# An output projection in column groups: low parts of the weights, residual loads, PSUM banks and gating in another order

## The chip, the core and the metric

The kernel runs on one core of a Trainium2 chip. The metric is the device time of one execution in microseconds (us). PE is the engine of the matmuls, DVE VectorE, ACT ScalarE, POOL GpSimd and SP SyncE; each works through its own instructions in order, and the DMAs that it issues stand in that order too. PSUM is the memory that PE writes to; the kernel uses it as eight banks of 128 partitions by 512 float32.

## What is computed

Two layers are applied to 640 tokens (128 context tokens and 512 latent ones), each 2048 wide. Per layer, with `h` the modulated input:

```python
shift, scale, gate = jnp.split(silu(cond) @ ada_w_l + ada_b_l, 3)
h = x * (1 + scale) + shift
z = h @ w_in_l
mix = concat([att * silu(ag), hg_out * silu(hgate), cv_out * silu(cgate)])
out = mix @ w_out_l                                  # (640, 2048) @ (2048, 2048)
x_new = layer_norm(ALPHA * x + gate * out, ln_w_l, ln_b_l)
```

This document is about the last two lines. `gate` and ALPHA scale the product and the residual `x`; the normalised result is the next layer's `x`, or the output.

## The kernel before, in words

Every large product is made with float32 accuracy from a high and a low part of each operand: `hi` is the operand rounded to float32r, `lo` is the operand minus `hi`, and three matmuls (HH by hi, HH by lo, HL by hi) are summed in PSUM. HH and HL hold the high and low parts of the activations for 5 token tiles (TT) and 16 steps of the contraction (KT). The layers follow each other: an input projection of 52 column tiles with the mixers' work beside it, then the output projection.

The **output projection** (lines 1411 to 1485) goes through 2048 output columns in five column groups, `GROUPS` (line 62): three of 512 columns (groups 0, 1, 2) and two of 256 (groups 3, 4). In groups 0 to 3 the loop of line 1417 takes the contraction step k outermost and the five token tiles inside, three matmuls each (line 1424), so five PSUM banks are open at once. Group 4 (lines 1460 to 1484) takes the token tiles outermost (line 1466), so that each tile can go on into the layer norm as soon as its 16 steps are done. A step k makes 15 matmuls.

**Weights.** `w_out` comes as 64 tiles of 128 x 512 a layer: 16 for each 512-wide group (a tile is a step k) and 8 for each 256-wide one (a tile is two steps). `o_load` (1143) loads a tile into one of the 8 RAW buffers on the SP queue. `o_split` (1149) makes hi and lo in two of the 16 WH buffers by `split_add` (288): ACT casts hi from RAW, ACT writes minus hi into lo, and POOL issues a DMA that adds the tile to lo once more from HBM. `feed` (1271) is called when a step has given its WH buffers back: it splits as many tiles as there are free pairs (so eight tiles are in flight) and loads until five are ahead of the split. RAW comes back after the cast.

**Work beside it in layer 0.** `ada_dve` (336) computes the next layer's modulation on DVE from 256 KB tiles (adawD) loaded on SP into the same RAW buffers. `pump(1, RWO)` after each step k (line 1430) lets it do RWO steps, and a step is two multiply-and-sum instructions of line 361 with their accumulator reads. With RWO = 1 that is 16 steps in each group. While five weight tiles are held, the three RAW buffers left let one ada tile be in flight at a time (line 343). In layer 1 there is no such work left.

**The residual.** `load_y` (1299) loads 128 tokens of `x` over all 2048 columns, 1 MB, on the POOL queue; the five of a layer are issued in group 0 after the steps 3, 5, 7, 9 and 11 (line 1431). In layer 1 `x` is the normalised value without weight and bias, and `affine` (1316) multiplies and adds them on DVE, from rows that `rows` (1306) loads on SP together with the gates. Those of group 0 are loaded at its start, those of each next group after step 9 of the group before; after step 13 of group 0 `affine` does groups 0 and 1, and after step 13 of the groups 1 to 3 the group that follows.

**Gating.** After step 15, `y_gate` (1326) multiplies each bank by the gate into a buffer, which is what gives the bank back; `y_add` (1332) then adds ALPHA times the residual and takes statistics (`bn_stats`). Both are on DVE, behind all that DVE was given in the group.

**PSUM banks** are taken from a queue (lines 1304, 1415, 1442): the four tiles m0 to m3 of one bank, then the two halves of each of the two-bank tiles z0 and z1, `free` being the halves of the one that the last input tile did not use. Five are taken per group and put back at its end, so a group begins with the three that its predecessor left, and the first pass over steps 0 and 1 does three token tiles before the other two (line 1418). In groups 1 and 3 the first bank so taken is the other half of a z tile whose first half the group before used for its last token tile.

**The end.** In layer 0 the tiles of group 4 are normalised, transposed and split into HH and HL (`ln_norm`, `ln_next`). In layer 1 `ln_out` (1395) normalises and stores the output.

Of the kernel before, what the change touches and what calls it, by code (L numbers as in the profile page):

```python
# [17 lines left out]
P = 128  # L18
D = 2048
KT = 16  # L20
T = 640
TT = 5
# [22 lines left out]
W0 = 4  # L45
WN = (0, 3, 4)
CY = 5
RWO = 1.0
WKEEP = 3
FL = 3  # L50
HF = 3
# [73 lines left out]
def trunk(ctx: ExitStack, tc: tile.TileContext, A: dict):  # L125
# [162 lines left out]
    def split_add(hi, lo, r, w):  # L288
        act.copy(hi, r)  # L289
        act.activation(lo, hi.bitcast(F32), AF.Copy, scale=-1.0)  # L290
        pool.dma_start(out=lo, in_=w.bitcast(F32R), accum_op=ALU.add)  # L291
# [857 lines left out]
    def o_split(l, t):  # L1149
        pump_until(lambda: len(WH.f) >= 2)  # L1150
        hi, lo = WH.take(), WH.take()
        r = oraw.pop((l, t))
        split_add(hi, lo, r, A["wout"][l, t])
        osp[l, OT[t][0], OT[t][1]] = (hi, lo)
        RAW.put(r)

# [57 lines left out]
    for l in range(DEPTH):  # L1214
# [81 lines left out]
        Y = yt["y"].rearrange("p (t n) -> p t n", t=TT)  # L1296
        xsrc = A["xr"] if l == 0 else n0

        def load_y(tt):
            pool.dma_start(out=Y[:, tt, :], in_=xsrc[128 * tt:128 * tt + 128, :])  # L1300

        zh = [z[:, h:h + 512] for z in zt for h in (0, 512)]
        free = [t[:, h:h + 512] for t in zt if t.tensor.name != z.tensor.name for h in (0, 512)]
        banks = deque(mb + free + [z[:, h:h + 512] for h in (0, 512)])

        def rows(gi):
            n0c, w = GROUPS[gi]
            src = [gsc[l, c] for c in range(2)] + ([A["lnw_r"][l - 1], A["lnb_r"][l - 1]] if l else [])
            out = []
            for r in src:  # L1310
                s = S.take()
                sync.dma_start(out=s[:, 0:w], in_=r[n0c:n0c + w].partition_broadcast(P))
                out.append(s)
            return out

        def affine(gi, gb):
            n0c, w = GROUPS[gi]
            for t in range(TT) if gi == 0 else (slice(0, TT),):
                yv = Y[:, t, n0c:n0c + w]
                for s, op in zip(gb[2:], (ALU.mult, ALU.add)):  # L1320
                    r = s[:, 0:w]
                    dve.tensor_tensor(yv, yv, r if gi == 0 else r.unsqueeze(1).to_broadcast([P, TT, w]), op=op)
            S.put(*gb[2:])
            del gb[2:]

        def y_gate(gi, tt, b, gb):
            w = GROUPS[gi][1]
            t = S.take()
            dve.tensor_tensor(t[:, 0:w], b[:, 0:w], gb[0 if tt == 0 else 1][:, 0:w], op=ALU.mult)  # L1329
            return t  # L1330
# [81 lines left out]
        gnext = None  # L1412
        for gi, (n0c, w) in enumerate(GROUPS[:-1]):
            gb = gnext or rows(gi)
            bs = [banks.popleft() for _ in range(TT)]
            kper = 512 // w
            for k0 in range(0, KT, 2):
                for tts, k in [(p, k) for p in ((range(3), range(3, TT)) if k0 == 0 else (range(TT),))
                               for k in (k0, k0 + 1)]:
                    hi, lo = osp[l, gi, k // kper]  # L1420
                    o = w * (k % kper)
                    for tt in tts:
                        for n_, (h_, w_) in enumerate(((HH, hi), (HH, lo), (HL, hi))):
                            pe.matmul(bs[tt][:, 0:w], lhsT=h_[:, tt, k, :], rhs=w_[:, o:o + w],  # L1424
                                      start=(k == 0 and n_ == 0), stop=(k == KT - 1 and n_ == 2))
                    if TT - 1 in tts:
                        if k % kper == kper - 1:
                            WH.put(*osp.pop((l, gi, k // kper)))
                            feed()
                        pump(1, RWO)  # L1430
                if gi == 0 and k0 in (2, 4, 6, 8, 10):
                    load_y(k0 // 2 - 1)
                if k0 == 8 and last:
                    gnext = rows(gi + 1)
                if k0 == 12 and last:
                    if gi == 0:
                        affine(gi, gb)
                    affine(gi + 1, gnext)
            ts = [y_gate(gi, tt, bs[tt], gb) for tt in range(TT)]
            for tt in range(TT):  # L1440
                y_add(gi, tt, ts[tt])
            banks.extend(bs)
            S.put(*gb)
        gi = len(GROUPS) - 1
        w = GROUPS[gi][1]
        gb = gnext or rows(gi)
        if last:
            cells = [RAW.take() for _ in range(8)]
            fin = [cells[0:4], cells[4:8]]
            for f, nm in zip(fin, ("lnw_r", "lnb_r")):  # L1450
                for q in range(4):
                    sync.dma_start(out=f[q], in_=A[nm][l, 512 * q:512 * q + 512].partition_broadcast(P))
        else:
            pump_until(lambda: not adaq)
            affine_consts()
            w_load(l + 1, 0)
            w_load(l + 1, 1)
            obank = [mb[0], zh[1], zh[3], zh[1], zh[3]]
            banks = deque(mb[1:] + mb[:1])
        for tt in range(TT):  # L1460
            b = banks.popleft() if last else obank[tt]
            for k in range(KT):
# [138 lines left out]
```

## Time and profile before

| | us |
|---|---|
| median of 3 runs (2290.06 to 2292.2) | 2291.16 |
| the profiled execution, its own time | 2289.98 |
| its span | 2288.2 |
| PE busy in the span | 2185.4 (96%) |
| DVE / ACT / POOL busy | 1393.0 / 1216.5 / 700.6 |
| output projection, layer 0, about | 928 to 1150 |
| output projection, layer 1, about | 2027 to 2284 |

Times in the rows are us from the start of the span. "Idle before" is the time that an engine stood still before an instruction, with the instruction that ended it. A busy share says how much of the time an engine had something to do; what a change can win is read from the waits of the engine that sets the pace in that stretch, here PE, and at the very end DVE.

### The profile page before, as it was taken

The numbers are of one execution on the slowest core, as the hardware profiler recorded it, in microseconds if no ns is written. First come the engines' busy times: TensorE is split into PE (matmuls) and PEld (weight loads), VectorE is DVE, ScalarE is ACT, GpSimd is POOL, SyncE is SP. The second block draws the span as 40 slices with busy tenths as digits, with TensorE's granted clock in tenths as the row PEclk, the third lists the DMA queues.
The fourth block names the chain that finished last, engine by engine and source line by source line (L and its number), as shares of the span: only waits on it lengthen the run. The fifth ranks groups of instructions, "written<-read, shape, count | busy, mean of one in ns | idle before, by whom it ended". The sixth has DMA issues, their size and how long they took to land. (4 is left out here: it accounts for less than half of the span.)

```text
span 2288.2 us, 42327 instructions
## 1 busy us (share of the span) xinstructions
PE 2185.4 (96%) x15854; PEld 2080.8 (91%) x15854; DVE 1393.0 (61%) x3647; ACT 1216.5 (53%) x2163; POOL 700.6 (31%) x790
## 2 busy tenths in 40 slices
PE   5899999999999999979989999999999999997996
PEld 3699999999999999868879999999999999996886
DVE  3488889557679998544473666534655786123227
ACT  1177877546564335623355878754656533552332
POOL 0034335322212333312232334433222224332225
PEclk9999999999999999989999999999999999998998
DMA  9968878887768789989835777678776667687884
GB/s 370 396 185 199 196 191 200 209 206 174 180 144 193 189 182 258 278 222 209 190 130 134 159 170 169 155 184 195 156 153 125 131 152 171 150 213 206 174 165 121
DMA packets 225663, 434.04 MB, mean 190 GB/s; under 512 B 26192, under 2 KB 32048, under 8 KB 223536
## 3 DMA queue, kind: packets, MB, share of 16 engines
q0 software_dynamic: 76544, 147.38, 37.7%
q1 hardware_dynamic: 138992, 271.85, 37.5%
q10 hardware_dynamic: 9920, 12.10, 1.6%
q8 instruction: 124, 2.03, 0.4%
q14 instruction: 83, 0.68, 0.1%
HBM read 413.87 MB, written 12.11 MB: 186 GB/s over the span
## 5 line engine op out<-in xcount | busy, mean ns | idle before, releaser
L1171 PE MATMUL z<-HH,wh 128*128 128x384 f32 x3296 | 1046.7, 339 | 0.0
L1169 PE MATMUL z<-HH,wh 128*128 128x256 f32 x3296 | 926.0, 283 | 1.1 <-DVE wh L286 0.9
L291 POOL DMA_DIRECT2D wh<-win x388 | 344.7, 934 | 1098.5 <-ACT wh L290 1017.0
L1169 PEld LDWEIGHTS z<-HH,wh 128*128 128x128 f32 x3296 | 619.0, 188 | 5.0 <-DVE wh L286 1.6
L1171 PEld LDWEIGHTS z<-HH,wh 128*128 128x128 f32 x3296 | 620.5, 188 | 1.5
L361 DVE SCALAR_TENSOR_TENSOR junk<-raw,s 128x256 bf16<-128x256 f32 x1024 | 502.5, 491 | 140.1 <-DMA raw<-adawD 111.9
L1171 PE MATMUL z<-HL,wh 128*128 128x384 f32 x1648 | 557.9, 339 | 0.0
L289 ACT CAST wh<-raw 128x512 fp32r<-128x512 f32 x516 | 316.1, 613 | 326.7 <-PE m L1424 131.1
L1169 PE MATMUL z<-HL,wh 128*128 128x256 f32 x1648 | 461.2, 280 | 0.0
L290 ACT ACTIVATE wh<-wh 128x512 fp32r<-128x512 f32 x516 | 326.4, 632 | 84.2 <-PE z L1171 69.5
L1169 PEld LDWEIGHTS z<-HL,wh 128*128 128x128 f32 x1648 | 310.6, 188 | 0.0
L1171 PEld LDWEIGHTS z<-HL,wh 128*128 128x128 f32 x1648 | 310.2, 188 | 0.0
L1026 DVE SCALAR_TENSOR_TENSOR s<-s,sm,s 128x655 f32<-128x655 f32 x240 | 229.0, 954 | 6.3
L291 POOL DMA_DIRECT2D wh<-wout x128 | 110.3, 862 | 347.1 <-ACT wh L290 336.2
L1424 PE MATMUL m<-wh,HH 128*128 128x512 f32 (+1 forms) x768 | 205.0, 354 | 0.0
L1424 PE MATMUL z<-wh,HH 128*128 128x512 f32 (+1 forms) x512 | 154.5, 384 | 29.8 <-DVE s L1329 28.4
L1424 PEld LDWEIGHTS m<-wh,HH 128*128 128x128 f32 x768 | 136.0, 189 | 19.8
L1424 PEld LDWEIGHTS z<-wh,HH 128*128 128x128 f32 x512 | 96.1, 193 | 49.3 <-issue 27.5
L1424 PE MATMUL m<-wh,HL 128*128 128x512 f32 (+1 forms) x384 | 135.8, 354 | 0.0
L1095 ACT ACTIVATE s<-z 128x640 f32<-128x640 f32 x32 | 22.5, 704 | 150.4 <-PE z L1171 141.6
L1424 PE MATMUL z<-wh,HL 128*128 128x512 f32 (+1 forms) x256 | 97.7, 382 | 0.0
L361 DVE DVE_READ_ACCUMULATOR junk<-raw,s 128x1 f32 x1024 | 83.5, 82 | 0.0
(555 smaller groups left out, 2661.0 us busy)
## 6 DMA issues: line engine op xcount, KB each, us to landing
raw<-win SPq DMA_DIRECT2D x416, 256.0 KB, 4.3
wh<-win POOLq DMA_DIRECT2D x388, 256.0 KB, 5.5
raw<-adawD SPq DMA_DIRECT2D x256, 256.0 KB, 4.2
x<-adaw SPq DMA_DIRECT2D x64, 512.0 KB, 8.2
raw<-wout SPq DMA_DIRECT2D x128, 256.0 KB, 5.0
wh<-wout POOLq DMA_DIRECT2D x128, 256.0 KB, 5.7
s<-crow SPq DMA_DIRECT2D x32, 256.0 KB, 6.2
s<-xT ACTq DMA_DIRECT2D x16, 320.0 KB, 7.1
```

Of the source, the lines that this page charges most:

```text
L289: act.copy(hi, r)
L290: act.activation(lo, hi.bitcast(F32), AF.Copy, scale=-1.0)
L291: pool.dma_start(out=lo, in_=w.bitcast(F32R), accum_op=ALU.add)
L361: dve.scalar_tensor_tensor(junk, r[:, 256 * n:256 * n + 256], 1.0, rows[0][:, 256 * c:256 * c + 256], op0=ALU.mult, op1=ALU.mult, accum_ou ...
L1026: dve.scalar_tensor_tensor(acc, u[:, t:t + AW], sm[:, cw + t:cw + t + 1], acc, op0=ALU.mult, op1=ALU.add)
L1095: act.activation(s[:, 0:T], zsb(z), AF.Silu)
L1169: pe.matmul(za, lhsT=w_, rhs=h_[:, 0:2, k, :], start=st_, stop=sp_)
L1171: pe.matmul(zb, lhsT=w_, rhs=h_[:, 2:5, k, :], start=st_, stop=sp_)
L1424: pe.matmul(bs[tt][:, 0:w], lhsT=h_[:, tt, k, :], rhs=w_[:, o:o + w], start=(k == 0 and n_ == 0), stop=(k == KT - 1 and n_ == 2))
```

## The change

Six edits, all in the output projection.

- From the seventh weight tile on (ODMA = 6) `o_split` calls `split`: ACT casts hi, and DVE subtracts hi from the loaded tile. Minus hi on ACT and the adding DMA go. RAW then comes back after the subtraction.
- `load_y` loads one column group of 128 tokens (512 columns, 256 KB; for group 3 the 512 columns of groups 3 and 4) after the steps 1, 3, 5, 7 and 9 of groups 0 to 3.
- `affine` is done for each group at its own step 11, per token tile; the rows are loaded at the group's start, and those of group 4 are loaded and used at step 11 of group 3, behind group 3's own.
- The banks are queued as m0, m1, the two `free` halves, m2, the two other halves, m3, and the last group's banks are chosen to match.
- After the steps 14 and 15 `feed` is not called; it is called once behind the five `y_gate`, ahead of `y_add`.
- RWO = 4/3 in the steps 0 to 11 and 0 in the steps 12 to 15: still 16 steps a group.

```diff
@@ -45,7 +45,8 @@
 W0 = 4
 WN = (0, 3, 4)
 CY = 5
-RWO = 1.0
+RWO = 4 / 3
+ODMA = 6
 WKEEP = 3
 FL = 3
 HF = 3
@@ -1150,7 +1151,10 @@
         pump_until(lambda: len(WH.f) >= 2)
         hi, lo = WH.take(), WH.take()
         r = oraw.pop((l, t))
-        split_add(hi, lo, r, A["wout"][l, t])
+        if t < ODMA:
+            split_add(hi, lo, r, A["wout"][l, t])
+        else:
+            split(hi, lo, r)
         osp[l, OT[t][0], OT[t][1]] = (hi, lo)
         RAW.put(r)
 
@@ -1296,12 +1300,16 @@
         Y = yt["y"].rearrange("p (t n) -> p t n", t=TT)
         xsrc = A["xr"] if l == 0 else n0
 
-        def load_y(tt):
-            pool.dma_start(out=Y[:, tt, :], in_=xsrc[128 * tt:128 * tt + 128, :])
+        def load_y(gi, tt):
+            n0c, w = GROUPS[gi]
+            w = w if gi + 2 < len(GROUPS) else 2 * w
+            if gi + 1 < len(GROUPS):
+                pool.dma_start(out=Y[:, tt, n0c:n0c + w], in_=xsrc[128 * tt:128 * tt + 128, n0c:n0c + w])
 
         zh = [z[:, h:h + 512] for z in zt for h in (0, 512)]
-        free = [t[:, h:h + 512] for t in zt if t.tensor.name != z.tensor.name for h in (0, 512)]
-        banks = deque(mb + free + [z[:, h:h + 512] for h in (0, 512)])
+        zf = [t[:, h:h + 512] for t in zt if t.tensor.name != z.tensor.name for h in (0, 512)]
+        zl = [z[:, h:h + 512] for h in (0, 512)]
+        banks = deque(mb[0:2] + zf + mb[2:3] + zl + mb[3:4])
 
         def rows(gi):
             n0c, w = GROUPS[gi]
@@ -1315,11 +1323,10 @@
 
         def affine(gi, gb):
             n0c, w = GROUPS[gi]
-            for t in range(TT) if gi == 0 else (slice(0, TT),):
+            for t in range(TT):
                 yv = Y[:, t, n0c:n0c + w]
                 for s, op in zip(gb[2:], (ALU.mult, ALU.add)):
-                    r = s[:, 0:w]
-                    dve.tensor_tensor(yv, yv, r if gi == 0 else r.unsqueeze(1).to_broadcast([P, TT, w]), op=op)
+                    dve.tensor_tensor(yv, yv, s[:, 0:w], op=op)
             S.put(*gb[2:])
             del gb[2:]
 
@@ -1412,6 +1419,7 @@
         gnext = None
         for gi, (n0c, w) in enumerate(GROUPS[:-1]):
             gb = gnext or rows(gi)
+            gnext = None
             bs = [banks.popleft() for _ in range(TT)]
             kper = 512 // w
             for k0 in range(0, KT, 2):
@@ -1426,25 +1434,29 @@
                     if TT - 1 in tts:
                         if k % kper == kper - 1:
                             WH.put(*osp.pop((l, gi, k // kper)))
-                            feed()
-                        pump(1, RWO)
-                if gi == 0 and k0 in (2, 4, 6, 8, 10):
-                    load_y(k0 // 2 - 1)
-                if k0 == 8 and last:
-                    gnext = rows(gi + 1)
-                if k0 == 12 and last:
-                    if gi == 0:
+                            if k0 < KT - 2:
+                                feed()
+                        pump(1, RWO if k0 < 12 else 0.0)
+                if k0 < 10:
+                    load_y(gi, k0 // 2)
+                if k0 == 10:
+                    if last:
                         affine(gi, gb)
-                    affine(gi + 1, gnext)
+                    if gi + 2 == len(GROUPS):
+                        gnext = rows(gi + 1)
+                        if last:
+                            affine(gi + 1, gnext)
             ts = [y_gate(gi, tt, bs[tt], gb) for tt in range(TT)]
+            feed()
             for tt in range(TT):
                 y_add(gi, tt, ts[tt])
             banks.extend(bs)
             S.put(*gb)
         gi = len(GROUPS) - 1
         w = GROUPS[gi][1]
-        gb = gnext or rows(gi)
+        gb = gnext
         if last:
+            banks = deque(mb[2:3] + zl[:1] + mb[3:4] + mb[0:2])
             cells = [RAW.take() for _ in range(8)]
             fin = [cells[0:4], cells[4:8]]
             for f, nm in zip(fin, ("lnw_r", "lnb_r")):
@@ -1455,8 +1467,8 @@
             affine_consts()
             w_load(l + 1, 0)
             w_load(l + 1, 1)
-            obank = [mb[0], zh[1], zh[3], zh[1], zh[3]]
-            banks = deque(mb[1:] + mb[:1])
+            obank = [mb[2], zh[1], zh[3], zh[1], zh[3]]
+            banks = deque(mb[3:] + mb[:3])
         for tt in range(TT):
             b = banks.popleft() if last else obank[tt]
             for k in range(KT):
```

## Rows read from the trace of the kernel before

**Rows 1.** Waits of PE, 920:1200 us (output projection, layer 0): total, times, longest.

```profile
PE z L1424 <- DVE s L1329: 15.0, 2, 13.3
...
PE m L1466 <- DMA wh<-wout: 1.8, 2, 1.2
```

**Rows 2.** Waits of PE, 2020:2289 us (output projection, layer 1).

```profile
PE z L1424 <- DVE s L1329: 13.4, 1, 13.4
...
PE z L1424 <- ACT wh L290: 1.4, 1, 1.4
```

**Rows 3.** Timeline of PE around the end of column group 0, layer 0 (start, duration).

```profile
982.47 0.39 PE L1424 MATMUL z<-wh,HL 128*128 128x512 f32 x1
996.16 1.19 PE L1424 MATMUL z<-wh,HH 128*128 128x512 f32 x2 [13.30 <-DVE s L1329]
...
1001.05 0.63 PE L1424 MATMUL z<-wh,HH 128*128 128x512 f32 x2
```

**Rows 4.** The same, layer 1.

```profile
2094.73 1.19 PE L1424 MATMUL z<-wh,HH 128*128 128x512 f32 x2 [13.39 <-DVE s L1329]
...
2099.87 0.62 PE L1424 MATMUL z<-wh,HH 128*128 128x512 f32 x2
```

**Rows 5.** Chain that ended last, layer 1: start, duration, what.

```profile
2064.34 2.72 PE m L1424 x12
...
2213.51 1.44 PE m L1424 x12
...
2271.26 1.71 DVE y1y L1407
```

**Rows 6.** Timeline of DVE, end of column group 0, layer 0.

```profile
992.12 0.42 DVE L361 SCALAR_TENSOR_TENSOR junk<-raw,s 128x256 bf16<-128x256 f32 x1 [4.18 <-DMA raw<-adawD]
...
992.94 2.48 DVE L1329 TENSOR_TENSOR s<-m,s 128x512 f32<-128x512 f32 x4
995.34 0.68 DVE L1329 TENSOR_TENSOR s<-z,s 128x512 f32<-128x512 f32 x1
```

**Rows 7.** Landing of adawD loads in column groups 0, 1, 2 of layer 0.

```profile
DMA to landing us min/median/max: 10.7/11.8/15.2
...
DMA to landing us min/median/max: 3.6/4.0/5.7
...
DMA to landing us min/median/max: 3.2/3.8/6.5
```

**Rows 8.** Timeline of DVE, layer 1, from column group 0 to the last one.

```profile
2084.58 7.01 DVE L1322 TENSOR_TENSOR y1y<-y1y,s 128x512 f32<-128x512 f32 x4 [6.14 <-DMA y1y<-n]
...
2214.20 1.48 DVE L1322 TENSOR_TENSOR y1y<-y1y,s 128x1280 f32<-128x1280 f32 x1
...
2235.15 0.42 DVE L1329 TENSOR_TENSOR s<-z,s 128x256 f32<-128x256 f32 x1 [16.75 <-PE z L1424]
...
2236.93 0.42 DVE L1335 SCALAR_TENSOR_TENSOR y1y<-y1y,s 128x256 f32<-128x256 f32 x1
...
2240.53 0.43 DVE L1337 BATCH_NORM_STATS2 bst<-y1y 128x6 f32<-128x256 f32 x1
2243.67 0.42 DVE L1329 TENSOR_TENSOR s<-z,s 128x256 f32<-128x256 f32 x1 [2.71 <-PE z L1466]
```

**Rows 9.** Issues of DMA: queue, count, size of one, median us to landing.

```profile
wh<-wout POOLq DMA_DIRECT2D x128, 256.0 KB, 5.7
...
y0y<-xr POOLq DMA_DIRECT2D x5, 1024.0 KB, 14.8
```

**Rows 10.** Timeline of DVE where it subtracts weight tiles already, from 1129 us.

```profile
1193.33 0.68 DVE L286 TENSOR_TENSOR wh<-raw,wh 128x512 fp32r<-128x512 f32 x1
```

**Rows 11.** Timeline of ACT and PE, last column groups of layer 1.

```profile
2232.99 0.62 ACT L289 CAST wh<-raw 128x512 fp32r<-128x512 f32 x1 [2.32 <-PE m L1424]
...
2236.39 0.40 PE L1466 MATMUL z<-wh,HH 128*128 128x256 f32 x2
```

**Rows 12.** Timeline of POOL, layer 0: the first residual load.

```profile
945.46 0.87 POOL L1300 DMA_DIRECT2D y0y<-xr  x1
```

## The prediction

> **What bounds the kernel now.** I read the waits of PE first, since PE is busy 96% of the span and only its waits can give much back, then the stretches around the long ones, then DVE and the DMAs that end them.
>
> In layer 0's output projection PE waits 15.0 us in two pieces for a DVE gate (13.3 and 1.7), and 1.8 us in group 4 for a weight tile's low part [rows 1]. In layer 1 it waits 13.4 us for a gate, and 1.4 us that the profile puts down to ACT [rows 2]; that piece is at the same place as layer 0's 1.7, the start of group 3. Both long pieces are the step from group 0 to group 1. The matmuls of 512 columns behind them are slow at first: from 996.16 to 1001.05 twelve of them take 4.89 us in layer 0 [rows 3], from 2094.73 to 2099.87 twelve take 5.14 us in layer 1 [rows 4], where twelve normally take 2.72 us [rows 5]. So each long wait costs 2.2 and 2.4 us more.
>
> Why is the gate late? In layer 0 DVE has an ada step ahead of it, and that step waited for its adawD tile; it starts at 992.12, ten us after PE's last matmul [rows 3, 6]. Such tiles land in 11.8 us in group 0, but in 4.0 and 3.8 us in the groups 1 and 2 [rows 7]. What group 0 has beside the others is five residual loads of 1 MB, landing in 14.8 us [rows 9]. In layer 1 DVE waits for the last of these loads itself and then does `affine` for the rest of group 0 and all of group 1, 7.0 us, ahead of the gates [rows 8].
>
> There is a second cause. Once DVE is free, PE starts at 996.16, after the fifth gate (995.34 plus 0.68), not after the first (992.94) [rows 3, 6]: group 1's first bank is the other half of the z tile that the fifth gate reads. The same pairing is at group 3, where the short waits are.
>
> **The change part by part.** I write E for the end of a group's last matmul. A step k is 15 matmuls: 3.40 us at 512 columns and 1.80 at 256 [rows 5].
>
> *Residual by column group.* Only 1.25 MB is needed by group 0's gates instead of 5.2 MB. POOL has nothing left in its queue that waits for PE once the adding DMAs are gone, so its twenty loads of a layer will not be spread over the groups: at 0.87 us of issue each [rows 12] they go out in 17 us, from about 945 to 963 in layer 0. I take the landing of adawD in that stretch as 11.8 us and behind it as 4.0 (ends: 3.6 and 15.2) [rows 7]. Five of group 0's 16 ada steps have their tiles by then. For the other 11 steps, five and a half tiles, one in flight: two landings of 11.8 and three and a half of 4.0, the latter each with two steps of 0.8 (992.12 to 992.94 [rows 6]), make 23.6 + 19.6 = 43 us counted one behind the other, to 988. PE needs the gate of the fourth token tile only at E + 4.1 (steps 0 and 1 of three token tiles, 18 matmuls of 0.227), at 986.8. So the stall is between nothing, as loads run one tile ahead, and about 2 us; a third slow landing adds 7.8. I take nothing: 13.3 + 2.2 us go in layer 0. In layer 1 there is no ada work; the first five loads, even one behind the other at 5.7 us [rows 9], are in after 29 us, and `affine` starts 41 us into group 0: ten operations of 0.6 to 0.7 us (1280 columns take 1.48 [rows 8]), done 5 us ahead of E. So 13.4 + 2.4 us go there.
>
> Small loads land in 5.7 us each and large ones in 14.8 [rows 9], so four small ones one behind the other are slower than one large one. The Trainium skill speaks against them too: "DMA: Bandwidth & Descriptors", section "Measured (HBM→SBUF, 128 partitions, SWDGE, issued from GpSimd)", says to batch DMAs to 1 MiB or more. Its fit for one DMA (section "Anatomy of one DMA — SWDGE (gpsimd) path": 2.0 us plus the bytes at 436 a ns) gives, as an estimate, 52 us for twenty of 256 KB against 22 for five of 1 MB; by that a layer would lose 30 us if nothing lay over it. The rows agree in direction.
>
> *Low parts on DVE.* 116 of 128 tiles lose minus hi on ACT and the adding DMA, and get 0.68 us of DVE [rows 10]. In layer 0 DVE then has per step k of a 512-wide group 0.7 for the tile and 4/3 of 0.8 for ada, 1.8 of 3.40 us; gates and adds of 10 us fall at the group's end, where ada pauses. The subtraction queues behind ada steps that wait for their tile, and PE is behind it only through `lo`; eight tiles in flight are 27 us of cover. RAW comes back one subtraction later, which SP's loads feel; five tiles are ahead. I cost this at nothing; the cover gone, see the last rival. In group 4 it pays: the last tile's `lo` no longer comes through a DMA of 5.7 us [rows 9] but 1.5 us behind its cast, so layer 0's 1.8 us go. DVE is ready there: gates 1.8, one subtraction 0.7, adds 4.0 [rows 8] and three small operations end at E + 6, where PE ends the first token tile.
>
> *Bank order, and gating ahead of subtractions.* Each group's first three banks then belong to no z tile that the group before gates last, and the gates no longer queue behind a subtraction that waits for step 15. So the pieces at group 3 go: 1.7 and 1.4 us. A gate that starts on time sits under the 4.1 us.
>
> *Rows and affine in group 3 of layer 1.* This costs. `affine` for the groups 3 and 4, 20 operations of 256 columns, now stands between step 11 and the gates of group 3. Step 11 ends at E - 7.2; cast and subtraction (0.24 + 0.62 + 0.68 [rows 10, 11]) bring DVE to E - 5.7. One operation is between 0.30 (1.48 over five, [rows 8]) and 0.42 (the nearest row, an operation of 256 columns on the same tile, [rows 8]); I take 0.42: 8.4, to E + 2.7. Then a subtraction 0.7, five gates 1.8, a subtraction 0.7, adds 4.0: E + 9.9. Before, the first gate of group 4 came at 2243.67, 7.3 us after group 4's first matmul [rows 8, 11]. From that gate on DVE's layer norm is the chain to the end [rows 5], so layer 1's end loses 2.6 us (0.1 with 0.30).
>
> **The sum.** Layer 0: 13.3 + 2.2 + 1.7 + 1.8 = 19.0. Layer 1: 13.4 + 2.4 + 1.4 - 2.6 = 14.6. Together 33.6. The profiled execution took 2289.98, which is 1.2 below the median: 2256.4, on the median's scale 2257.6. I say 2256. About 0.2%, 4.6 us, is what a measurement of this kernel can tell from no change. Own range: 2251 (affine cheap, restarts of PE a few tenths each) to 2265 (a slow landing in group 0 of layer 0, and the median's 1.2).
>
> **Rivals.**
>
> *The burst holds layer 0's gate.* If ada tiles keep landing at 11.8 us until group 0 ends, because the twenty residual loads last that long, DVE is late as now, and 15.5 us stay: 2272. For: 11.8 was measured under just such loads [rows 7]. Against: they are issued 20 us ahead of the group's end. Chance 0.07. (The page's 52 us from 945 on is such a case.) If layer 1's wait stays too, because the residual comes as late, 31.3 of 33.6 stay: 2288, no change; 0.04.
>
> *The banks do not come apart.* If PE still waits for all five gates at the groups' starts, each of two starts a layer costs the last gate, 0.7 plus 0.2, 3.6 us in all: 2260. Chance 0.05. For it: four waits fit a dependence on the tile, but no row shows the tracking itself.
>
> *DVE becomes the bound: slower.* RAW is freed by DVE, SP's load waits for RAW, DVE's ada step waits for the load, and the next subtraction stands behind it. With three buffers for both, a load uses a buffer freed about two steps k before it lands, so two steps last at least landing + 0.8 + 0.5. At 4.0 us this is 2.7 us a step, under PE's 3.40. At 11.8 it is 6.6: twelve steps 79 us, four without ada 6, so 85 against 54.4 us a group; three groups lose 92 less 27 of cover, 65, against 34 won: 2321. It decides from where the twelve steps take more than 48 us, a landing of 6.7 us in the groups 1 and 2. Against: 4.0 and 3.8 there, 6.5 at most [rows 7], with fewer DMAs afterwards. Chance 0.06.
>
> **How the numbers follow.** Forecast 0.78, rivals 0.07, 0.04, 0.05 and 0.06. Faster: 0.78 + 0.07 + 0.05 = 0.90; same 0.04; slower 0.06. The range runs from 2250 to 2272: the forecast's own with the 1.2, reached out to the case of one stall left; what is outside is the no-change case, the slower one and some of the forecast's tails, under 0.2.
>
> **What would show it.** Right: no wait of PE over 2 us between groups, no stretch of slow matmuls in either layer's group 1, adawD landing long only in the first 20 us of group 0, residual loads bunched behind each other on POOL, and the first gate of group 4 in layer 1 some 10 us after E with PE waiting for DVE. Wrong: a gate of group 0 later than E + 4 in layer 0, PE waiting for a `wh` subtraction, or twenty residual loads spread over the groups with `affine` waiting for one of them.

## The result, and the profile after

| us | before | after |
|---|---|---|
| median (4 runs each) | 2290.61 (2289.07 to 2292.2) | 2253.64 (2252.99 to 2254.24) |
| ratio of the times, 95% interval | | 0.9838, 0.9821 to 0.9856 |
| span of the profiled execution | 2288.2 | 2251.1 |
| DVE / ACT / POOL busy | 1393.0 / 1216.5 / 700.6 | 1472.3 / 1142.6 / 616.0 |
| moved by DMA, MB | 434.04 | 403.60 |

The span is 37.1 us shorter; 33.6 were forecast for the profiled execution. On another chip the two kernels gave 2254.35 against 2291.87, ratio 0.9836 (0.9822 to 0.9849).

The best single view is the busy time of the engines from the first matmul of column group 0 to the first one of group 4, a row for each layer. The columns are the stretch, its length, the busy time and count of PE, PEld (PE's loads of weights), DVE, ACT and POOL, the granted clock as a share of 2.4 GHz, the DMA share and GB/s. The kernel before:

```profile
928.25:1137.86 209.61, 194.63 (x962) 165.29 (x961) 89.28 (x307) 79.90 (x129) 53.65 (x64) 0.97 0.89 221
2026.77:2236.39 209.62, 194.84 (x961) 165.47 (x961) 63.05 (x93) 79.88 (x129) 53.66 (x64) 0.97 0.83 192
```

The changed kernel:

```profile
928.27:1120.27 192.00, 192.00 (x961) 163.93 (x961) 121.98 (x361) 44.01 (x72) 12.43 (x22) 1.00 0.54 168
2006.02:2198.05 192.03, 192.03 (x961) 163.92 (x961) 99.21 (x172) 44.03 (x72) 12.46 (x22) 1.00 0.43 132
```

After the change PE is busy in every microsecond of both stretches, at the full clock. No wait is left in it, so 192.0 us is taken as the floor of this stretch for these matmuls, and everything above it in another kernel is called loss: 17.6 us a layer before. That gives 35.2 of the 37.1. From group 4 of layer 0 to the start of layer 1's output projection 888.9 became 885.8, 3.1 less (this stretch took 885.6 to 887.1 in two executions of the change and two of a version that differs only in group 3, e8 and e12 below, so between 1.8 and 3.3). From group 4 of layer 1 to the end 51.8 became 53.1, 1.3 more: the one place where the change costs.

The waits of PE, 900 to 1200 us, changed kernel: neither line is of the projection's matmuls (L1385 transposes in the layer norm, L1173 is the next input projection). In layer 1's output projection PE has no wait at all. This stands against [rows 1, 2].

```profile
PE m L1385 <- ACT s L1392: 6.1, 6, 3.9
PE z L1173 <- DVE wh L287: 0.9, 1, 0.9
```

DVE at the end of group 0, layer 0, which answers to [rows 6]:

```profile
976.54 0.42 DVE L362 SCALAR_TENSOR_TENSOR junk<-raw,s 128x256 bf16<-128x256 f32 x1
...
976.89 1.28 DVE L287 TENSOR_TENSOR wh<-raw,wh 128x512 fp32r<-128x512 f32 x2
980.16 1.37 DVE L1336 TENSOR_TENSOR s<-m,s 128x512 f32<-128x512 f32 x2 [1.99 <-PE m L1432]
982.20 1.29 DVE L1336 TENSOR_TENSOR s<-z,s 128x512 f32<-128x512 f32 x2 [0.67 <-PE z L1432]
983.40 0.68 DVE L1336 TENSOR_TENSOR s<-m,s 128x512 f32<-128x512 f32 x1
984.00 1.28 DVE L287 TENSOR_TENSOR wh<-raw,wh 128x512 fp32r<-128x512 f32 x2
```

The last ada step is done by 977, the gates now wait for PE (1.99 and 0.67) instead of PE for them, and the subtractions for the last steps' weight buffers (984.00) stand behind the gates. The adawD tiles, as in [rows 7] for the groups 0, 1 and 2:

```profile
DMA to landing us min/median/max: 2.8/6.4/13.0
...
DMA to landing us min/median/max: 2.5/2.9/4.3
...
DMA to landing us min/median/max: 2.5/2.7/4.1
```

POOL's residual loads in layer 0, against [rows 12]: eight at once, then most of them when an earlier one has landed, twenty in 18.8 us.

```profile
941.24 4.28 POOL L1307 DMA_DIRECT2D y0y<-xr  x8 [7.52 <-issue]
945.84 0.54 POOL L1307 DMA_DIRECT2D y0y<-xr  x1 [0.32 <-DMA y0y<-xr]
...
959.45 0.54 POOL L1307 DMA_DIRECT2D y0y<-xr  x1 [0.57 <-DMA y0y<-xr]
```

DVE in layer 1: `affine` of group 0, then the end of group 3 up to the first gate of group 4, against [rows 8]:

```profile
2048.32 6.73 DVE L1329 TENSOR_TENSOR y1y<-y1y,s 128x512 f32<-128x512 f32 x10
...
2192.31 8.04 DVE L1329 TENSOR_TENSOR y1y<-y1y,s 128x256 f32<-128x256 f32 x20
2200.27 0.69 DVE L287 TENSOR_TENSOR wh<-raw,wh 128x512 fp32r<-128x512 f32 x1
2200.87 1.08 DVE L1336 TENSOR_TENSOR s<-m,s 128x256 f32<-128x256 f32 x3
...
2202.53 0.68 DVE L287 TENSOR_TENSOR wh<-raw,wh 128x512 fp32r<-128x512 f32 x1
...
2207.08 0.41 DVE L1336 TENSOR_TENSOR s<-m,s 128x256 f32<-128x256 f32 x1
```

Group 4's first matmul is at 2198.05, so its first gate comes 9.0 us later; it was 7.3 in [rows 8, 11]. PE does not wait for it: its five token tiles have five banks, and PE is busy without a gap from 2198 to 2227.

### The profile page after: what moved, and what is told of

Read it like the earlier page. It is cut to its first block, busy times and chain, and to the rows that moved or that the text cites. A ratio compares the mean times of both kernels' runs of the same rounds, so it can differ in the third digit from the quotient of the medians.

```text
span 2251.1 us, 42122 instructions
## 1 busy us (share of the span) xinstructions
PE 2178.7 (97%) x15854; PEld 2077.2 (92%) x15854; DVE 1472.3 (65%) x3795; ACT 1142.6 (51%) x2047; POOL 616.0 (27%) x704
## 2 busy tenths in 40 slices
DMA packets 210716, 403.60 MB, mean 179 GB/s; under 512 B 24816, under 2 KB 30672, under 8 KB 209872
## 4 chain that ended last, share of the span: by engine, by line
PE 77%; DVE 11%; DMA 4%; issue 3%; ACT 3%; POOL 1%; ACTq 0%; SPq 0%; DVEq 0%; POOLq 0%
PE z L1175 31%; PE z L1173 21%; PE z L1432 9%; PE m L1432 8%; DVE junk L362 4%; DMA x<-adaw 2%; PE m L948 2%; PE m L862 2%; PE m L916 1%; DMA s<-xT 1%; PE m L664 1%; DVE y1y L1414 1%; ACT s L1392 1%; DVE s L534 1%; DVE y1y L1415 0%
## 5 line engine op out<-in xcount | busy, mean ns | idle before, releaser
L1173 PE MATMUL z<-HH,wh 128*128 128x256 f32 x3296 | 926.4, 283 | 1.6 <-DVE wh L287 0.9
L1173 PEld LDWEIGHTS z<-HH,wh 128*128 128x128 f32 x3296 | 619.4, 189 | 5.5 <-DVE wh L287 1.6
L1173 PE MATMUL z<-HL,wh 128*128 128x256 f32 x1648 | 461.3, 280 | 0.0
L1173 PEld LDWEIGHTS z<-HL,wh 128*128 128x128 f32 x1648 | 311.0, 189 | 0.0
L291 ACT ACTIVATE wh<-wh 128x512 fp32r<-128x512 f32 x400 | 253.1, 633 | 79.4 <-PE z L1175 68.4
L290 ACT CAST wh<-raw 128x512 fp32r<-128x512 f32 x400 | 244.0, 610 | 71.2 <-issue 36.2
L286 ACT CAST wh<-raw 128x512 fp32r<-128x512 f32 x136 | 83.0, 621 | 305.0 <-PE m L1432 156.6
L1432 PE MATMUL z<-wh,HH 128*128 128x512 f32 (+1 forms) x640 | 182.0, 368 | 0.0
L1432 PE MATMUL m<-wh,HH 128*128 128x512 f32 (+1 forms) x640 | 173.8, 357 | 0.0
L287 DVE TENSOR_TENSOR wh<-raw,wh 128x512 fp32r<-128x512 f32 x138 | 92.6, 687 | 122.9 <-ACT wh L286 120.2
L1432 PEld LDWEIGHTS z<-wh,HH 128*128 128x128 f32 x640 | 116.1, 189 | 20.0
L1432 PEld LDWEIGHTS m<-wh,HH 128*128 128x128 f32 x640 | 114.1, 189 | 17.5
L1432 PE MATMUL z<-wh,HL 128*128 128x512 f32 (+1 forms) x320 | 117.7, 368 | 0.0
L1432 PE MATMUL m<-wh,HL 128*128 128x512 f32 (+1 forms) x320 | 114.3, 357 | 0.0
```

The source lines that it names most:

```text
L286: act.copy(hi, src)
L287: (lo_eng or dve).tensor_tensor(lo, src, hi.bitcast(F32), op=ALU.subtract)
L1173: pe.matmul(za, lhsT=w_, rhs=h_[:, 0:2, k, :], start=st_, stop=sp_)
```

## The experiments

The six edits are taken as four parts: the residual with its `affine`, the banks, the low parts, and the gating (`feed` behind the gates, and RWO). Each part was made alone on the kernel before, and each was left out of the changed kernel. "Loss" is the time from the first matmul of group 0 to the first of group 4 less 192.0; "tail" is from the latter, in layer 1, to the end of the span. Both come from PE's timeline of the profiled execution. The ratio is the kernel's time over that of the kernel before on the same chip; savings in us taken from it differ by up to 1.3 from those of the medians.

| kernel | ratio (95%) | loss, layer 0 | loss, layer 1 | tail |
|---|---|---|---|---|
| before | 1 | 17.6 | 17.6 | 51.8 |
| residual alone (e1) | 0.9876 (0.9859 to 0.9893) | 6.2 | 2.8 | 51.5 |
| banks alone (e2) | 0.9940 (0.9920 to 0.9960) | 10.5 | 9.1 | 51.5 |
| low parts alone (e9) | 0.9999 (0.9990 to 1.0008) | 19.4 | 20.5 | 51.1 |
| gating alone (e10) | 0.9958 (0.9944 to 0.9971) | 9.0 | 16.3 | 51.3 |
| all (after) | 0.9838 (0.9821 to 0.9856) | 0.0 | 0.0 | 53.1 |
| all but banks (e3) | 0.9858 (0.9843 to 0.9873) | 2.8 | 2.8 | 54.6 |
| all but residual (e4) | 0.9841 (0.9827 to 0.9856) | 0.0 | 5.3 | 51.0 |
| all but low parts (e5) | 0.9839 (0.9825 to 0.9852) | 0.0 | 0.0 | 54.1 |
| all but gating (e6) | 0.9841 (0.9827 to 0.9854) | 1.6 | 0.8 | 53.0 |
| all, subtractions twice (e7) | 0.9840 (0.9826 to 0.9853) | 0.0 | 0.0 | 55.2 |
| all, affine of groups 3, 4 earlier (e8) | 0.9815 (0.9802 to 0.9828) | 0.0 | 0.0 | 50.1 |

### The residual alone

```diff
-            pool.dma_start(out=Y[:, tt, :], in_=xsrc[128 * tt:128 * tt + 128, :])
+                pool.dma_start(out=Y[:, tt, n0c:n0c + w], in_=xsrc[128 * tt:128 * tt + 128, n0c:n0c + w])
...
-                if gi == 0 and k0 in (2, 4, 6, 8, 10):
-                    load_y(k0 // 2 - 1)
+                if k0 < 10:
+                    load_y(gi, k0 // 2)
```

`affine` goes with it, as in the change; banks, low parts and gating are those of before.

> The kernel before with one part of the change alone: residual and affine by column group. Theory (group 0's gate was late because of what the residual's loads and affine put ahead of it): both waits of 13 us go; what stays is the wait for the z tile's other half at the groups 1 and 3, 1.4 to 1.7 us each as group 3 shows it now, layer 0's 1.8 us in group 4, and layer 1's end loses about half a us more than it wins: 2290.6 - 31.3 + 3.4, about 2263. Rival (ada's loads are late for another reason than the residual): layer 0's wait of 13 us stays, about 2278. Rival (the adding DMAs on POOL's queue still space the loads, so the residual of group 0 comes late for layer 1's affine): layer 1's stays.

Measured: 2264.45 where before took 2293.79, so 28 us less by the ratio and 29 by the medians. The theory held in the main; neither rival did. PE's waits in layer 0's projection:

```profile
PE z L1427 <- DVE s L1331: 3.0, 1, 3.0
...
PE m L1470 <- DMA wh<-wout: 1.7, 2, 1.4
PE z L1427 <- ACT wh L290: 1.4, 1, 1.4
```

The wait of 13.3 in layer 0 is 3.0 (1.4 to 1.7 were expected), that of 13.4 in layer 1 is 0.9, the piece at group 3 (here put down to ACT) stays at 1.4, and the low part through the DMA still holds group 4. This part alone is three quarters of the gain.

### The order of banks alone

```diff
-        banks = deque(mb + free + [z[:, h:h + 512] for h in (0, 512)])
+        banks = deque(mb[0:2] + zf + mb[2:3] + zl + mb[3:4])
...
-            obank = [mb[0], zh[1], zh[3], zh[1], zh[3]]
+            obank = [mb[2], zh[1], zh[3], zh[1], zh[3]]
```

> The kernel before with the new bank order alone. Theory (PE waits for the fifth gate because of the shared z tile): group 1 now starts on three banks that no gate holds and needs the first two gates only 4.1 us later; of 13.3 us the 4.1 and the three later gates (1.8) go, about 6 in each layer, and the 1.7 and 1.4 us at group 3: 15 us in all, 2275. A wait of some 7 us stays per layer, on an m bank. Rival (the tile is not what PE waits for): the waits stay at 13 us, 2290.

Measured: 2278.72 where before took 2293.79. PE waits 8.1 us in layer 0 and 6.2 in layer 1, now for a gate of an `m` bank, once a layer:

```profile
PE m L1425 <- DVE s L1330: 8.1, 1, 8.1
PE m L1468 <- DMA wh<-wout: 2.5, 2, 2.1
```

The waits for `z` tiles, at group 1 and at group 3, are gone. The theory held, and the pairing of halves was the second cause: PE now goes through the first two steps of three token tiles before it needs a bank whose gate is late, and it waits for that gate alone.

### The change with the old banks

The opposite of that edit, on the changed kernel.

> The changed kernel with the bank order of before. Theory: at the starts of the groups 1 and 3 PE waits for the last of five gates that are on time, 1 to 1.4 us each, four in all: 4 to 5.5 us over the changed kernel, 2258 to 2259. Rival (with gates on time the order is of no matter): 2253.6, no waits at the groups' starts.

Measured: 2260.96; 0.9838 of this chip's 2293.79 would be 2256.6, so 4.3 us more, with intervals that overlap; the spans differ by 8.7. The waits come back, two of them in each layer's groups and 5.6 us in group 4 of layer 1:

```profile
PE z L1431 <- DVE s L1335: 2.3, 2, 1.4
...
PE z L1476 <- DVE s L1335: 5.6, 2, 3.4
```

The loss is 2.8 a layer, the tail 1.5 longer; the latter was not expected. In this kernel the banks are worth about a third of what they are worth alone, since the gates come on time.

### The change with the old residual

```diff
+            pool.dma_start(out=Y[:, tt, :], in_=xsrc[128 * tt:128 * tt + 128, :])
...
+                if gi == 0 and k0 in (2, 4, 6, 8, 10):
+                    load_y(k0 // 2 - 1)
...
+                if k0 == 12 and last:
+                    if gi == 0:
+                        affine(gi, gb)
+                    affine(gi + 1, gnext)
```

> The changed kernel with the residual as before: five loads of 1 MB in group 0, affine of group 0 and 1 after step 13. Theory as I forecast it (what group 0 has to load decides): waits come back in both layers, 10 to 13 us each, about 2275 to 2280. Rival (since the adding DMAs are gone nothing spaces the loads, so the 5.2 MB come as early as they do now, and only layer 1's order of affine costs): layer 0 as the changed kernel; in layer 1 affine of two groups ends 7 us after group 0's last matmul, a wait of 5 us and 2 of slow clock, less 2 us won at the end where affine stands earlier: 2258 to 2260.

Measured: 2257.28 where before took 2293.79. **The theory fell; the rival held in its mechanism.** (By the ratio, 0.9841 against 0.9838, the time cannot be told from the change; the median lies 0.7 below the rival's range.) The 1 MB loads do not bring layer 0's wait back: its loss is 0.0. They leave POOL together at the start of group 0, where before they went out one by one from 945 to 971, each behind adding DMAs that wait for ACT and PE:

```profile
941.92 2.64 POOL L1304 DMA_DIRECT2D y0y<-xr  x5 [7.51 <-issue]
```

They land in 12.7 us (median), and adawD in group 0 in 3.7, less than with the small loads (6.4). What it costs is layer 1's order: `affine` for two groups ahead of the first gate. The chain around the end of group 0 in layer 1:

```profile
2063.16 2.83 DVE y1y L1327
2065.99 0.02 issue
2066.01 2.83 DVE y1y L1327
2068.83 0.61 DVE s L1334
2069.49 4.28 PE m L1429 x12
```

The gate is done 7.6 us after the group's end (2061.8), and PE, which can run 4.3 us into group 1 without it, waits 3.4 and runs slowly after that. Of the 5.3 that layer 1 loses, 2.1 come back at the end, where `affine` for the last groups stands earlier (tail 51.0 in place of 53.1).

### The change with low parts by DMA

```diff
-ODMA = 6
+ODMA = 64
```

> The changed kernel with the low parts of all tiles by the adding DMA, as before. Theory (DVE's subtraction pays only in group 4; elsewhere eight tiles in flight hide either way): layer 0's wait of 1.8 us in group 4 comes back, layer 1's end wins the two subtractions that stand ahead of its gates (1.3 us), the residual's loads are spaced by POOL again: 2254 to 2256. Rival (taking the adding DMAs off is what lets ada's tiles land early): adawD lands in 5 us or more in the groups 0 to 2, a gate of layer 0 is late, 5 us or more: 2259 and above.

Measured: 2255.72 where before took 2293.19. Ratio 0.9839 against 0.9838: no difference that can be told. The adding DMAs are back in POOL's queue, adawD lands in 7.2, 6.4 and 5.3 us in the groups 0, 1 and 2 in place of 6.4, 2.9 and 2.7, and PE waits 1.3 and 0.9 us for a low part in group 4. With the small residual and the new banks all this is covered. The 1.3 us that the expectation gave back at layer 1's end did not come: the tail is 1.0 longer.

### The change with the old gating

```diff
-RWO = 4 / 3
+RWO = 1.0
...
-                            if k0 < KT - 2:
-                                feed()
-                        pump(1, RWO if k0 < 12 else 0.0)
+                            feed()
+                        pump(1, RWO)
             ts = [y_gate(gi, tt, bs[tt], gb) for tt in range(TT)]
-            feed()
```

> The changed kernel with the order of before inside a group: feed after every step and none behind the gates, one ada step after each step k. Theory (a gate has 4.1 us of cover, and a subtraction that waits for step 15 delays it by 1.5): no wait of PE returns, 2253 to 2255. Rival (gates queue behind the subtraction and an ada step that waits for its tile): 2 us or more at each of three groups' ends, 2258 and above.

Measured: 2256.69 where before took 2293.19. Waits of 1.3 us in layer 0 and 0.5 in layer 1 return, more than the theory's none and less than the rival's 2 at each group's end; the ratio does not tell it from the change.

### The change with every subtraction of a weight tile twice

```diff
             split(hi, lo, r)
+            dve.tensor_tensor(lo, r, hi.bitcast(F32), op=ALU.subtract)
```

> The changed kernel with each of the 116 subtractions made twice on DVE: the suspected cost doubled, 39 us more of DVE a layer. Theory (hidden by the tiles in flight): only what stands ahead of the first gate of group 4 shows, 1.2 us in layer 1 and as much in layer 0: 2255 to 2256.5. Rival (DVE has become the bound of the stage): 10 us or more, PE waiting for wh.

Measured: 2256.58, ratio 0.9840 (0.9826 to 0.9853). 116 more operations, 80 us of DVE, cost one wait of 2.0 us in group 4 of layer 1, where the tail is 2.1 longer, and nothing in the groups 0 to 3. DVE is not near being the bound there.

### The affine of groups 3 and 4 earlier

```diff
+                end = gi + 2 == len(GROUPS)
+                if k0 < (2 if end else 10):
+                    for tt in range(TT) if end else (k0 // 2,):
+                        load_y(gi, tt)
+                if end and k0 == (2 if last else 10):
+                    gnext = rows(gi + 1)
+                if k0 == (6 if end else 10) and last:
+                    affine(gi, gb)
+                    if end:
+                        affine(gi + 1, gnext)
```

> The changed kernel with group 3's residual loaded at its start and affine of the groups 3 and 4 of layer 1 after step 7 in place of step 11. Theory (it stands ahead of the gates and DVE's backlog sets the end): the first gate of group 4 comes when PE is done, 6 us after group 3's last matmul in place of 9: 3 us less, about 2250.5. Rival (the end is set by something else, or the operations are late for another wait): 2253.6.

Measured: 2251.06, ratio 0.9815. It was run once more beside the changed kernel, on another chip:

> The changed kernel itself once more, beside the next run on the same chip: 0.984 of the kernel before, 2254 to 2257.

> The changed kernel with group 3's residual loaded at its start and affine for the groups 3 and 4 behind step 7, once more beside the changed kernel on one chip. Theory (the 20 operations ahead of group 3's gates are the one thing of the change that costs, about 3 us): 2.5 to 4 us under the changed kernel of the same call, the two intervals against the kernel before barely touching. Rival (the gain of the earlier run was the chip's): within 1 us of it.

Measured there: 2254.35 (2253.02 to 2255.47) for the change and 2250.76 (2249.49 to 2252.13) for the earlier affine, 3.6 us less with ranges that do not touch; the ratios to the kernel before, 0.9836 (0.9822 to 0.9849) and 0.9822 (0.9808 to 0.9835), have intervals that overlap. The tail is 50.1 in both of its profiled executions, 53.1 and 53.0 in those of the change. In the second pair, DVE's timeline with the earlier affine (group 4's first matmul at 2197.60):

```profile
2184.66 8.04 DVE L1329 TENSOR_TENSOR y1y<-y1y,s 128x256 f32<-128x256 f32 x20
...
2196.36 1.15 DVE L1336 TENSOR_TENSOR s<-m,s 128x256 f32<-128x256 f32 x3 [0.81 <-PE m L1432]
...
2203.56 0.42 DVE L1336 TENSOR_TENSOR s<-m,s 128x256 f32<-128x256 f32 x1 [0.46 <-PE m L1479]
```

The same 20 operations, 7.2 us earlier as counted from group 4's first matmul, and the first gate of group 4 comes 6.0 us behind the group's first matmul, where it waits for PE and not PE's work for it. So the place of those 20 operations is what the change costs, about 3 us, and **this version beats both kernels**.

### The low parts alone

```diff
-        split_add(hi, lo, r, A["wout"][l, t])
+        if t < ODMA:
+            split_add(hi, lo, r, A["wout"][l, t])
+        else:
+            split(hi, lo, r)
```

> The kernel before with the low parts of 116 weight tiles on DVE, nothing else. Theory (with no adding DMA in POOL's queue nothing spaces the residual loads, so this part alone frees layer 0's gate): the five 1 MB loads go out near 942, all within 3 us; adawD lands around 4 us in the median of group 0; layer 0's 13.3 us and its slow matmuls go, the 1.7 us of the bank pairing stays, 1.8 us of group 4 go. In layer 1 affine for the groups 0 and 1 stays ahead of the gates: 5 to 7 us of wait in place of 13.4, then some slow matmuls. Median 2263 to 2270 where before is 2292. Rival (only the smaller residual, not the missing DMAs, frees the gate): PE waits over 10 us for layer 0's gate and the time is 2285 to 2290.

Measured: 2291.34 against 2291.87, ratio 0.9999 (0.9990 to 1.0008): no difference. The theory was right about the loads and wrong about the time. As it says, POOL sends the five loads at once at 941.37, and adawD lands in 3.6 us in group 0. The rival did not hold either: it had PE wait over 10 us. DVE, at the end of group 0 (PE's last matmul starts at 982.62), and then PE have this:

```profile
983.70 0.69 DVE L287 TENSOR_TENSOR wh<-raw,wh 128x512 fp32r<-128x512 f32 x1 [1.89 <-ACT wh L286]
984.31 0.42 DVE L362 SCALAR_TENSOR_TENSOR junk<-raw,s 128x256 bf16<-128x256 f32 x1
...
985.12 2.48 DVE L1333 TENSOR_TENSOR s<-m,s 128x512 f32<-128x512 f32 x4
987.51 0.68 DVE L1333 TENSOR_TENSOR s<-z,s 128x512 f32<-128x512 f32 x1
```

```profile
988.34 1.19 PE L1428 MATMUL z<-wh,HH 128*128 128x512 f32 x2 [5.33 <-DVE s L1333]
```

The subtraction waits for a cast of ACT, which waits for the weight buffer of the step just ended; two instructions of ada follow, then four gates, and only the fifth frees the `z` tile. PE waits 5.33 us, and 5.33 again at group 3, where it waited 1.7. In layer 1 twelve operations of affine and two subtractions stand ahead of the gates:

```profile
2076.09 12.32 DVE L1326 TENSOR_TENSOR y1y<-y1y,s 128x512 f32<-128x512 f32 x12
2088.33 1.29 DVE L287 TENSOR_TENSOR wh<-raw,wh 128x512 fp32r<-128x512 f32 x2
2089.54 2.47 DVE L1333 TENSOR_TENSOR s<-m,s 128x512 f32<-128x512 f32 x4
```

PE waits 11.2 us there, where 5 to 7 were expected. The old wait is gone, and others in the same places have taken its place: moving the subtraction to DVE puts it ahead of the gates in a queue that works in order. With the gating of the change (e3) or its banks (e6), both beside the small residual, layer 0's loss is 2.8 and 1.6 in place of 19.4.

### The gating alone

The opposite of the edit in the section on the old gating, on the kernel before.

> The kernel before with the ada pause of the last steps (4/3 step a step until step 11, none behind it) and the weight feed behind the gates, nothing else. Theory (the pause only moves the same 16 ada steps together, and each still waits for a tile that lands late under the residual loads; layer 1 has no ada work): PE's wait for layer 0's gate stays between 8 and 15 us, layer 1's at 13 us; median 2284 to 2292. Rival (the pause alone puts the gates on time in layer 0): no wait over 2 us there, 15 us less, 2275 to 2278.

Measured: 2283.04, ratio 0.9958. Neither: layer 0's wait is 4.6 us, below the theory's 8 and above the rival's 2; layer 1's is 12.5, as said. Before, the sixth adawD load of group 0 was issued at 981.3; asked for 4/3 as often, it goes out at 974.3, and the last ada step starts at 983.89 in place of 992.12 [rows 6]:

```profile
983.89 0.43 DVE L361 SCALAR_TENSOR_TENSOR junk<-raw,s 128x256 bf16<-128x256 f32 x1 [2.47 <-DMA raw<-adawD]
...
984.71 2.48 DVE L1329 TENSOR_TENSOR s<-m,s 128x512 f32<-128x512 f32 x4
```

```profile
987.93 1.19 PE L1424 MATMUL z<-wh,HH 128*128 128x512 f32 x2 [4.63 <-DVE s L1329]
```

The expectation overlooked that an earlier request moves the whole row of landings forward, though each still takes 10.1 us in the median.

### What follows from all of them

Alone, the four parts give 28, 14, 0 and 10 us (1 less the ratio, times the kernel before on that chip): 52 in sum, where the whole gives 37. Left out one at a time, each is missed by 5 us at most, and no ratio is clear of the change's interval. They do not add up because they work on the same few waits: a gate comes late, and PE needs its bank at once. Of the 17.6 us that each layer lost, an early gate removes 11.4 and 14.8 alone (residual) or 8.6 and 1.3 (gating), and a bank not needed at once 7.1 and 8.5 (banks). The residual and the banks together without the other two were not tried.

## Why the prediction was right, and where its steps were off

The forecast of 2256 is 2.4 us above the median of 2253.64. Every place at which it saw time won or lost is where time was won or lost; the saving came out 3.5 us larger than the sum because four terms were off in the same direction. The account of what causes layer 0's long wait held only in part.

- *Layer 0's long wait goes* (13.3 + 2.2) and *the pieces at group 3 go* (1.7 and 1.4). Shown: no loss is left in either layer. The terms add up to 17.2 a layer, and 17.6 were lost; the 0.4 is small losses at the waits that the sum left out.
- *The working for layer 0's ada was too slow.* The counting put the last ada step near 988 and the gate within 2 us of PE's need. It started at 976.54, 11 us earlier. Not all tiles before 963 took 11.8: the median in group 0 was 6.4, and in group 1 it was 2.9, not 4.0. The working left the stall between nothing and about 2 us; that nothing was taken was a choice, and it came out right because the tiles landed faster than it assumed.
- *The cause named for it was only half of the story.* The text put the slow tiles down to the five 1 MB loads. With these loads and without adding DMAs (e4) the wait does not return, since the loads go out together, 40 us before the group's end. So the 15.5 us that the sum books under the residual are not the residual's alone; that the sum came out is in part because the change also took away the adding DMAs. The tiles are slow wherever the loads are spaced out behind adding DMAs (in the median 11.8 us in the kernel before, 10.1 in e10, and still 9.2 with small loads in e1), and fast where the large loads go out together without them (3.6 in e9, 3.7 in e4). No run has the spacing without the adding DMAs, so how much of this is the spacing and how much the adding DMAs' own transfers is not shown. The burst itself, 945 to 963 forecast, was 941 to 960 and landed by about 967.
- *Small loads against large.* The prediction held, as a rival, that twenty small loads might last too long. By the fit of the Trainium skill, "DMA: Bandwidth & Descriptors", section "Anatomy of one DMA — SWDGE (gpsimd) path", one behind the other they would take an estimated 52 us. The trace gives about 26, from the first issue at 941.24 to 7.4 (the median landing) behind the last at 959.45, as several are in flight at once; against the five large ones (e4) no loss of time is seen in layer 0, whose loss is 0.0 with either. The 5.7 us that the prediction took for a small load is the row of the adding DMAs; the small residual loads themselves took 7.4.
- *Layer 1's wait goes* (13.4 + 2.4). Shown: `affine` of group 0 starts 42 us into the group (41 forecast), takes 6.7 us and ends 5.5 ahead of the group's end (5 forecast).
- *Group 4 of layer 0* (1.8). The DMA wait is gone. The stretch from there to layer 1's output projection is 3.1 shorter. Of what goes beyond 1.8, 1.1 is in the transposes' waits for ACT (7.2 to 6.1), which were 6.9 in the change's second execution, so it is not told from what the stretch varies by.
- *Rows and affine at the end of layer 1* (2.6 lost). The mechanism was right, to the start of affine: E - 5.7 was forecast, and 2192.31 is E - 5.7. The 20 operations took 8.04, 0.40 each and not 0.42, the two subtractions and the gates some tenths less, so the gate came at E + 9.0 in place of E + 9.9; the loss is 1.7 there and 1.3 at the end of the span. The term was mis-sized by 1.3. The earlier affine (e8, e12) takes it away, which shows the cause. Two things were overlooked. In the kernel before, 1.1 of the 7.3 us was PE's wait for a low part by DMA, which the change removes as in layer 0; this is most of why the version with the earlier affine has a shorter tail than the kernel before (50.1 against 51.8). And PE was forecast to wait for DVE there; it does not, and the loss is on DVE's chain alone.
- *Rivals.* No gate of group 0 is late. The banks do come apart, and e3 shows what it would have been otherwise, 2.8 a layer against 1.8 worked out. DVE as the bound falls: adawD lands in 2.9 and 2.7 us in the groups 1 and 2, against the 6.7 from which it decides, and twice the subtractions are hidden too (e7).
- *Low parts at no cost* holds within the change, where leaving them out cannot be measured (e5); alone they move the waits to other places (e9). The prediction named the gates' queueing behind a subtraction that waits for step 15, but gave it no price of its own, and it gave the parts' sum without saying which parts could stand in for each other.

## What to carry to other kernels

When an engine waits for a result, list what stands ahead of that result in its producer's queue and how soon the consumer needs the buffer; work for later (the next group's affine, weights or modulation) belongs behind it, and the first buffers taken should be those given back first. Test parts both alone and left out: 52 us of single gains here were 37 together, and a part that could not be measured within the change (the low parts) brought new waits of 5.3 and 11.2 us when it stood alone. When the waits are gone, look at what was moved in front of the last chain of the kernel, since nothing covers it there: 3.0 us at the last group's first gate were 3.0 us of the span here (e8).

## What was not expected of the hardware

What the slow matmuls behind a wait cost is much the same for a wait of 5 us and for one of 13. The granted clock in the stretch right behind the wait, in the kernel before, layer 1 (13.4 us of wait), then e9, layer 0 (5.3), e4, layer 1 (3.4), and e3, layer 0 (1.4); columns as in the first fences:

```profile
2094.73:2100.00 5.27, 5.27 (x13) 4.16 (x14) 5.13 (x12) 0.00 (x0) 0.00 (x0) 0.53 0.01 3
```

```profile
988.34:994.30 5.96, 5.96 (x14) 4.70 (x15) 5.82 (x13) 0.00 (x0) 0.00 (x0) 0.51 0.50 176
```

```profile
2069.49:2073.80 4.31, 4.31 (x13) 3.44 (x14) 4.28 (x8) 0.62 (x1) 0.00 (x0) 0.67 0.11 19
```

```profile
1095.15:1099.00 3.85, 3.85 (x32) 3.85 (x33) 3.78 (x9) 0.00 (x0) 0.00 (x0) 1.00 0.14 25
```

0.53 and 0.51 are nearly all at 1.2 GHz, 0.67 is part at 1.2 and part at 2.4, 1.00 is all at 2.4. Counted from start to start against 0.227 us a matmul, the 13.4 us wait cost 2.4 us more, the one of 5.3 cost 2.9 (18 matmuls in 6.9 us instead of 4.1), the one of 3.4 cost 1.8, and behind the one of 1.4 there is no slow stretch. The other runs fit in: 3.0 us of wait cost 1.4 (e1), 4.6 cost 2.5 (e10), 6.2 and 8.1 cost 2.7 and 2.3 (e2), 11.2 cost 2.0 (e9), 12.5 cost 2.0 (e10). A wait of three to five microseconds is therefore dearer than it looks in the list of waits, by about half of itself.

An issue of a residual load takes POOL 0.54 us, not the 0.87 of [rows 12]: in the kernel before, the loads of 0.87 to 0.89 us start while the issue of an adding DMA (0.86) is still under way, and the one that does not took 0.55. Behind the first eight loads of layer 0 POOL waits 0.3 to 0.7 us (once 3.9) before the next, by the profile mostly for a landing; in layer 1, too, eight go out at once and the waits behind them are 0.2 to 1.1.
